# Scores of the differential attention as matmuls over 64 rows, two maps on the two halves of TensorE's rows

## The chip, the cores and the metric

The kernel runs on one core of a Trainium2 chip. The metric is the device time of one execution in microseconds; the time before is the median of three runs, 740.84 us (739.97 to 741.19). All tensors are float32; matmuls take float32 operands rounded to the type fp32r.

## What is computed

One encoder block over 512 tokens of width 1024: a joint projection, two attentions side by side, gates, an output projection, a SwiGLU channel mixer and a final norm. The change touches the second attention, which has 4 heads with two maps each, of 64 dimensions:

```python
bq = apply_rope(bq.reshape(b, s, B_HEADS, 2, HEAD_DIM).transpose(0, 2, 3, 1, 4), ang_1d)
bk = apply_rope(bk.reshape(b, s, B_HEADS, 2, HEAD_DIM).transpose(0, 2, 3, 1, 4), ang_1d)
...
sc = jnp.einsum('bhcqd,bhcsd->bhcqs', qi, k).astype(jnp.float32) * scale
p = jax.nn.softmax(sc, axis=-1)
diff = (p[:, :, 0] - lam * p[:, :, 1]).astype(v.dtype)
return jnp.einsum('bhqs,bhse->bhqe', diff, v)
```

The index c is the map. Each score is a product over 64 numbers, and there are 2 x 512 x 512 scores for each head.

## The kernel before

To keep accuracy, an operand is split into a high part (rounded to fp32r, on ScalarE, line 73) and a low part (the rest, on VectorE, line 80). A projection takes three matmuls for each block: high by high, high by low, low by high (`mm3`, lines 93 to 95).

`group_b(h)` makes one head of the second attention. It loads four units of weights, and for each of four token tiles (128 tokens) it projects to 384 columns (128 of q, 128 of k, 128 of v; tile `acc_b`), scales into `z`, splits v, applies the rotary embedding and packs q and k with `pack_heads`. A packed row holds for each of q map 0, q map 1, k map 0, k map 1 the 64 high and the 64 low numbers side by side, and for k a third part, the unsplit 64 numbers again (line 247). TensorE transposes these pieces of 128 columns (line 254, tile `pt_b`): q as high over low, k once as high over low and once as low over whole. That is six transposes for each token tile, in two PSUM tiles of four and two, and three copies to SBUF on ScalarE (line 256).

`attend_b(h)` goes over the four token tiles. `probs` makes one map's scores of 128 queries by 512 keys with two matmuls over all 128 rows (line 353): the first adds high by high and low by low, the second high by low and low by high. Then come the maximum (VectorE, line 355), the exponential with its sum (ScalarE, line 358) and the reciprocal (line 360). Tiles `sc_b_0x` to `sc_b_3x` are the first map's scores of the four token tiles, `sc_b_0y` to `sc_b_3y` the second map's. All scores share two PSUM banks (`ps_sc`), so a score matmul waits until the exponential of the tile two scores earlier has read its bank. The two maps are joined, the result is transposed (line 366, `ptp_b`), split and multiplied with v (`mm3`, tile `ob`).

The heads are woven: `attend_b(0)` runs with `group_b(2)`, `attend_b(1)` with `group_b(3)`, `attend_b(2)` and `attend_b(3)` with the gate columns (`gate_col`, tile `gt`, matmuls of 512 columns), while the first attention (`attend_a`) has `group_b(1)` and two gate columns between its heads. The program text is not the order of execution: a scheduler that works with a simulated timeline draws the order of each engine's queue, and TensorE then runs its queue strictly in that order.

Of the kernel before, what the change touches and what calls it, by code (L numbers as in the profile page):

```python
# [37 lines left out]
def kernel(  # L38
# [33 lines left out]
    def split_hi(dst, src):  # L72
        a.copy(dst, src)  # L73
# [5 lines left out]
    def split_lo(dst, src, hi):  # L79
        v.tensor_tensor(out=dst, in0=src, in1=hi.bitcast(F32), op=ALU.subtract)  # L80
# [122 lines left out]
    def do_rope(q4, tab, tt, nm):  # L203
        cos_, sin_ = tab
        n, nh = q4.shape[1], q4.shape[2]
        w = n * nh * HD

        def flat(tag):
            t = tmp.tile([P, S], F32, tag=tag, name=f"{tag}_{nm}")[:, :w]
            return t, t.rearrange("p (n h d) -> p n h d", h=nh, d=HD)  # L210

        def bc(t, c):
            return t[:, tt:tt + n, c].unsqueeze(2).to_broadcast([P, n, nh, c.stop - c.start])

        r, r4 = flat("t1")
        t, t4 = flat("t2")
        v.tensor_tensor(out=r4, in0=q4, in1=bc(cos_, slice(0, HD)), op=ALU.mult)
        for h in range(2):
            c, o = slice(32 * h, 32 * h + 32), slice(32 - 32 * h, 64 - 32 * h)
            g.tensor_tensor(out=t4[:, :, :, c], in0=q4[:, :, :, o], in1=bc(sin_, c), op=ALU.mult)  # L220
        v.tensor_tensor(out=r, in0=r, in1=t, op=ALU.add)
        return r.rearrange("p (h d) -> p h d", d=HD)
# [14 lines left out]
    def u_tile(nm, dt=F32R, shape=(P, 2, S)):  # L237
        return up.tile(list(shape), dt, tag="u", name=nm)

    def pack_heads(r3, nh, nk, nm):  # L240
        qs = tmp.tile([P, 8 * P], F32R, tag="qs", name=f"qs_{nm}")
        w = 3 * HD if nk else P
        qs = qs[:, :nh * w].rearrange("p (h w) -> p h w", w=w)
        split_hi(qs[:, :, 0:HD], r3)
        split_lo(qs[:, :, HD:P], r3, qs[:, :, 0:HD])
        if nk:
            v.tensor_copy(qs[:, nh - nk:, P:], r3[:, nh - nk:, :])
        return qs

    def transpose_heads(srcs, dsts, tt, nm, av=False):  # L250
        pt = ps_av.tile([P, S], F32, tag="av", name=f"pt_{nm}") if av else ps_hd.tile([P, S], F32, tag="hd", name=f"pt_{nm}")
        ptr = pt.bitcast(F32R)
        for j, src in enumerate(srcs):
            pe.transpose(out=ptr[:, j * P:(j + 1) * P], in_=src, identity=identr)
        for i, dst in enumerate(dsts):
            a.copy(dst[:, :, tt * P:(tt + 1) * P], pt[:, 2 * i * P:(2 * i + 2) * P].rearrange("p (j t) -> p j t", t=P))

    def pair(qs, h):
        return [qs[:, h, 0:P], qs[:, h, HD:HD + P]]
# [65 lines left out]
    def group_b(h, parts):  # L325
        us = [load_unit(w_in[6 + 4 * h + u, :, :768], f"b{h}_{u}", 768) for u in range(4)]
        vt = u_tile(f"vb{h}", shape=(P, NT, 2, P))
        qT = u_tile(f"qTb{h}")
        kT = [u_tile(f"kTb{h}_{i}") for i in range(2)]
        for tt in range(NT):  # L330
            nm = f"b{h}_{tt}"
            t = slice(tt * P, (tt + 1) * P)
            acc = ps_mm.tile([P, S], F32, tag="mm", name=f"acc_{nm}")[:, :384]
            for kt in range(KT):
                hi, lo = us[kt // 2]
                o = (kt % 2) * 384
                mm3(acc, xgh[:, kt, t], xgl[:, kt, t], hi[:, o:o + 384], lo[:, o:o + 384], kt == 0, kt == KT - 1)
            z = tmp.tile([P, S], F32, tag="q", name=f"z_{nm}")
            a.activation(z[:, :128], acc[:, :128], AF.Copy, scale=rstd8[:, tt:tt + 1])
            a.activation(z[:, 128:384], acc[:, 128:384], AF.Copy, scale=rstd[:, tt:tt + 1])  # L340
            split_hi(vt[:, tt, 0, :], z[:, 256:384])
            split_lo(vt[:, tt, 1, :], z[:, 256:384], vt[:, tt, 0, :])
            qs = pack_heads(do_rope(z[:, :256].rearrange("p (n h d) -> p n h d", n=1, d=HD), tabs["b"], tt, nm), 4, 2, nm)
            transpose_heads([qs[:, 0, 0:P], qs[:, 1, 0:P]] + pair(qs, 2), [qT, kT[0]], tt, f"{nm}_0")
            transpose_heads(pair(qs, 3), [kT[1]], tt, f"{nm}_1")
            if tt == NT - 1:
                parts[:] = [qT, kT, vt]
            yield True

    def probs(ql, kT, tt, nm):  # L350
        sc = ps_sc.tile([P, S], F32, tag="sc", name=f"sc_{nm}")
        for i in range(2):
            pe.matmul(sc, lhsT=ql[:, tt * P:(tt + 1) * P], rhs=kT[:, i, :], start=i == 0, stop=i == 1)
        nm_ = small.tile([P, 1], F32, tag="nmax", name=f"nmax_{nm}")
        v.tensor_reduce(out=nm_, in_=sc, op=ALU.max, axis=AX.X, negate=True)  # L355
        pr_ = pp.tile([P, S], F32, tag="p", name=f"p_{nm}")
        s_ = small.tile([P, 1], F32, tag="psum", name=f"s_{nm}")
        a.activation(pr_, sc, AF.Exp, bias=nm_, scale=1.0, accum_out=s_)  # L358
        r_ = small.tile([P, 1], F32, tag="prec", name=f"r_{nm}")
        v.reciprocal(out=r_, in_=s_)  # L360
        return pr_, r_
# [11 lines left out]
    def attend_a(qT, kT, vt, fillers):  # L373
        for h in range(8):
            kv = h // 4
            if h >= 2:
                fillers[h - 2]()
            ps = []
            for tt in range(NT):
                nm = f"a{h}_{tt}"  # L380
                p_, r_ = probs(qT[h // 2][:, h % 2, :], kT[kv], tt, nm)
                g.tensor_scalar(out=p_, in0=p_, scalar1=r_, scalar2=1.0, op0=ALU.mult, op1=ALU.mult)  # L382
                ps.append(p_)
            av = ps_av.tile([P, S], F32, tag="av", name=f"oa_{h}")
            for kt in range(NT):
                ph, pl = transpose_p(ps, kt, f"a{h}_{kt}")
                pe.matmul(av, lhsT=vt[:, kt, kv, :], rhs=ph, start=kt == 0, stop=False)
                pe.matmul(av, lhsT=vt[:, kt, kv, :], rhs=pl, start=False, stop=kt == NT - 1)
            if h % 4 == 0:
                oA.append(u_tile(f"oA{kv}", F32))  # L390
            low = tmp.tile([HD, S], F32, tag="avt", bufs=1, name=f"low_{h}")
            a.copy(low, av[HD:P, :])
            v.tensor_tensor(out=oA[kv][HD * (h % 2):HD * (h % 2) + HD, h % 4 // 2, :], in0=av[0:HD, :], in1=low, op=ALU.add)

    def attend_b(h, qT, kT, vt):
        ps = []
        for tt in range(NT):
            nm = f"b{h}_{tt}"
            p0, r0 = probs(qT[:, 0, :], kT[0], tt, nm + "x")
            g.tensor_scalar(out=p0, in0=p0, scalar1=r0, scalar2=1.0, op0=ALU.mult, op1=ALU.mult)  # L400
            p1, r1 = probs(qT[:, 1, :], kT[1], tt, nm + "y")
            c1 = small.tile([P, 1], F32, tag="c1", name=f"c1_{nm}")
            v.tensor_tensor(out=c1, in0=r1, in1=nlam, op=ALU.mult)
            v.scalar_tensor_tensor(out=p0, in0=p1, scalar=c1, in1=p0, op0=ALU.mult, op1=ALU.add)
            ps.append(p0)
            yield True
        av = ps_av.tile([P, S], F32, tag="av", name=f"ob_{h}")
        for kt in range(NT):
            ph, pl = transpose_p(ps, kt, f"b{h}_{kt}")
            mm3(av, vt[:, kt, 0, :], vt[:, kt, 1, :], ph, pl, kt == 0, kt == NT - 1)  # L410
            yield True
        if h % 2 == 0:
            oB.append(u_tile(f"oB{h // 2}", F32))
        o = oB[h // 2][:, h % 2, :]
        a.copy(o, av)
        sq = tmp.tile([P, S], F32, tag="avt", bufs=1, name=f"sqb_{h}")
        a.activation(sq, av, AF.Square)
        pn = ps_tp.tile([P, S], F32, tag="tp", name=f"pn_{h}")
        for tt in range(NT):
            pe.matmul(pn[:, tt:tt + 1], lhsT=sq[:, tt * P:(tt + 1) * P], rhs=ones, start=True, stop=True)  # L420
        rs = small.tile([P, NT], F32, tag="rsb", name=f"rsb_{h}")
        rsqrt_mean(rs, pn[:, 0:NT], P, NT)
        pb = ps_tp.tile([P, S], F32, tag="tp", name=f"pb_{h}")
        for tt in range(NT):
            pe.matmul(pb[:, tt * P:(tt + 1) * P], lhsT=rs[:, tt:tt + 1].to_broadcast([P, P]), rhs=ident, start=True, stop=True)
        v.scalar_tensor_tensor(out=o, in0=o, scalar=gsub, in1=pb, op0=ALU.mult, op1=ALU.mult)
# [579 lines left out]
```

## Time and profile before

| | |
|---|---|
| median of three runs | 740.84 us |
| profiled execution | 741.09 us |
| its span, first to last instruction | 739.3 us |
| matmuls on TensorE | 4335 |
| mean granted clock of TensorE | 0.993 |
| VectorE, ScalarE, GpSimd busy | 545.3, 420.0, 174.3 us |

The second attention's scores run between 160 and 280 us of the span, its projections and transposes between 76 and 255 us. A busy time in the profile counts each matmul from its start to its modelled end, and consecutive matmuls overlap; what one costs in a full queue is read from the distance between starts.

### The profile page before, as it was taken

Reading aid. Unit: us, or ns where it says so; the run is one execution under the profiler, and the core shown is the slowest. Engines: PE = TensorE matmul, PEld = TensorE weight load, DVE = VectorE, ACT = ScalarE, POOL = GpSimd, SP = SyncE. Lnnn points to the kernel's source line nnn. Section 1 sums busy time; section 2 is a strip of 40 time slices with the busy share of each in tenths; the row PEclk is TensorE's granted clock in tenths of the full one; section 3 lists DMA queues with packets and bytes.
Section 4 is the critical chain, followed back from the end, with each engine's and each line's share of the span. In section 5 each row is a group of like instructions: output and inputs, shape, how many; then the busy total and the mean of one; then the engine's idle time right before and its main releaser. Section 6 shows DMA issues by size and latency. Waiting matters only on the chain.

```text
span 739.3 us, 11815 instructions
## 1 busy us (share of the span) xinstructions
PE 717.8 (97%) x4335; PEld 644.3 (87%) x4335; DVE 545.3 (74%) x917; ACT 420.0 (57%) x755; POOL 174.3 (24%) x223
## 2 busy tenths in 40 slices
PE   5899999999999999999999999999999999999996
PEld 5789978789998888888889989999999999988885
DVE  5787778859987565557447967878887888778884
ACT  6355687967677666432326635555555555546672
POOL 3656433335662220100000022211212120110002
PEclk9899999999999999999999999999999999999999
DMA  8215708068979652433413397876687773559973
GB/s 315 94 44 184 244 22 271 21 133 197 235 171 244 139 138 72 152 107 112 143 58 106 98 317 217 242 207 178 215 253 194 234 184 125 172 180 321 339 241 115
DMA packets 48634, 129.95 MB, mean 176 GB/s; under 512 B 5600, under 2 KB 6496, under 8 KB 48576
## 3 DMA queue, kind: packets, MB, share of 16 engines
q1 hardware_dynamic: 34736, 95.57, 38.0%
q0 software_dynamic: 11248, 28.19, 19.5%
q10 hardware_dynamic: 2592, 5.45, 2.1%
q8 instruction: 34, 0.56, 0.3%
q14 instruction: 24, 0.20, 0.1%
HBM read 119.87 MB, written 32.37 MB: 206 GB/s over the span
## 4 chain that ended last, share of the span: by engine, by line
PE 92%; DMA 3%; DVE 2%; ACT 1%; issue 1%; SPq 0%; POOL 0%; POOLq 0%; ACTq 0%; DVEq 0%
PE q L95 5%; PE q L94 5%; PE q L93 5%; PE gt L94 4%; PE gt L93 4%; PE gt L95 4%; PE p L95 4%; PE p L93 4%; PE p L94 4%; PE acc_b L93 3%; PE acc_b L94 3%; PE acc_b L95 3%; PE r L94 2%; PE r L93 2%; PE r L95 2%; PE pp L93 2%
## 5 line engine op out<-in xcount | busy, mean ns | idle before, releaser
L95 PE MATMUL gt<-xgh,wlo_g 128*128 128x512 f32 x128 | 50.6, 395 | 0.0
L94 PE MATMUL gt<-xgl,whi_g 128*128 128x512 f32 x128 | 50.5, 394 | 0.0
L93 PE MATMUL gt<-xgh,whi_g 128*128 128x512 f32 x128 | 50.4, 394 | 0.0
L691 POOL DMA_DIRECT2D x<-in_w_x_dram x18 | 16.2, 899 | 126.5 <-DMA x<-in_w_x_dram 53.9
L94 PE MATMUL acc_b<-wlo_b,xgh 128*128 128x384 f32 x128 | 43.6, 340 | 0.0
L93 PE MATMUL acc_b<-whi_b,xgh 128*128 128x384 f32 x128 | 43.5, 340 | 0.0
L95 PE MATMUL acc_b<-whi_b,xgl 128*128 128x384 f32 x128 | 43.4, 339 | 0.0
L768 POOL DMA_DIRECT2D sd<-s x44 | 28.2, 670 | 51.6 <-DVE s L765 24.8
L382 POOL TENSOR_SCALAR p_a<-p_a,r_a 128x512 f32<-128x512 f32 x32 | 23.6, 740 | 51.1 <-DVE r_a L360 43.6
L73 ACT CAST whi_a<-raw_a 128x1024 fp32r<-128x1024 f32 x18 | 18.9, 1050 | 21.1 <-issue 11.7
L80 DVE TENSOR_TENSOR wlo_t<-raw_t,whi_t 128x1024 fp32r<-128x1024 f32 (+1 forms) x24 | 27.0, 1130 | 4.0 <-ACT whi_t L73 3.9
L73 ACT CAST sh<-sr 128x512 fp32r<-128x512 f32 (+1 forms) x30 | 17.5, 583 | 21.6 <-PE p L94 7.8
L73 ACT CAST whi_y<-y 128x1024 fp32r<-128x1024 f32 x18 | 18.9, 1050 | 19.1 <-PE p2d L95 15.4
L93 PE MATMUL p<-whi_t,sh 128*128 128x512 f32 (+1 forms) x77 | 27.4, 360 | 1.0 <-DVE x L860 1.0
L80 DVE TENSOR_TENSOR wlo_y<-y,whi_y 128x1024 fp32r<-128x1024 f32 x18 | 22.0, 1221 | 8.7 <-ACT whi_y L73 8.7
L95 PEld LDWEIGHTS gt<-xgh,wlo_g 128*128 128x128 f32 x128 | 24.0, 188 | 4.8
L94 PEld LDWEIGHTS gt<-xgl,whi_g 128*128 128x128 f32 x128 | 24.0, 188 | 4.8
L93 PEld LDWEIGHTS gt<-xgh,whi_g 128*128 128x128 f32 x128 | 24.1, 188 | 4.8
L358 ACT ACTIVATE p_a<-sc_a,nmax_a 128x512 f32<-128x512 f32 x32 | 22.5, 703 | 8.8 <-DVE nmax_a L355 7.9
L94 PE MATMUL p<-wlo_t,sh 128*128 128x512 f32 (+1 forms) x77 | 26.9, 359 | 0.0
L220 POOL TENSOR_TENSOR t_b<-z_b,csb 128x128 f32<-128x128 f32 x32 | 23.8, 763 | 11.6 <-ACT z_b L340 10.1
L95 PE MATMUL p<-whi_t,sl 128*128 128x512 f32 (+1 forms) x77 | 26.1, 360 | 0.1
(390 smaller groups left out, 2734.2 us busy)
## 6 DMA issues: line engine op xcount, KB each, us to landing
td<-in_w_down_dram SPq DMA_DIRECT2D x20, 512.0 KB, 8.1
raw_t<-td SPq DMA_DIRECT2D x20, 512.0 KB, 4.6
x<-in_w_x_dram SPq DMA_DIRECT2D x18, 512.0 KB, 4.9
raw_a<-in_w_gu_dram SPq DMA_DIRECT2D x18, 512.0 KB, 5.1
x<-in_w_x_dram POOLq DMA_DIRECT2D x18, 512.0 KB, 5.9
raw_g<-in_w_in_dram SPq DMA_DIRECT2D x16, 512.0 KB, 6.1
sr<-sd SPq DMA_DIRECT2D x25, 256.0 KB, 4.4
raw_b<-in_w_in_dram SPq DMA_DIRECT2D x16, 384.0 KB, 3.8
```

The source lines that it names most:

```text
L73: a.copy(dst, src)
L80: v.tensor_tensor(out=dst, in0=src, in1=hi.bitcast(F32), op=ALU.subtract)
L93: pe.matmul(acc, lhsT=lh, rhs=rh, start=start, stop=False, skip_group_check=loose)
L94: pe.matmul(acc, lhsT=lh, rhs=rl, start=False, stop=False, skip_group_check=loose)
L95: pe.matmul(acc, lhsT=ll, rhs=rh, start=False, stop=stop, skip_group_check=loose)
L220: g.tensor_tensor(out=t4[:, :, :, c], in0=q4[:, :, :, o], in1=bc(sin_, c), op=ALU.mult)
L358: a.activation(pr_, sc, AF.Exp, bias=nm_, scale=1.0, accum_out=s_)
L382: g.tensor_scalar(out=p_, in0=p_, scalar1=r_, scalar2=1.0, op0=ALU.mult, op1=ALU.mult)
L691: g.dma_start(x, w_x1[f], accum_op=ALU.add)
L768: g.dma_start(sdram[i][p][:, k, :], t)
```

## The change

`pack_heads` is no longer used for the second attention. `pack_pairs` packs the two maps side by side: 128 columns of high parts (64 of map 0, 64 of map 1) and 128 of low parts, for q and for k. Transposed, map 0 lies on rows 0 to 63 and map 1 on rows 64 to 127. Four transposes in one PSUM tile and two copies are left for each token tile, and k has one tile instead of two. `scores_pair` takes both score banks and makes the scores of both maps with three matmuls each over 64 rows: high by high, high by low, low by high; it writes them in turn, map 0, map 1, map 0 and so on. Low by low is no longer computed. `probs` is split so that it takes a finished score tile.

```diff
--- before.py
+++ after.py
@@ -245,6 +245,16 @@
         split_lo(qs[:, :, HD:P], r3, qs[:, :, 0:HD])
         if nk:
             v.tensor_copy(qs[:, nh - nk:, P:], r3[:, nh - nk:, :])
+        return qs
+
+    def pack_pairs(r3, nh, nm):
+
+        qs = tmp.tile([P, 8 * P], F32R, tag="qs", name=f"qs_{nm}")[:, :2 * nh * HD]
+        qs = qs.rearrange("p (s j w) -> p s j w", s=2, w=P)
+        r3 = r3.rearrange("p (j h) d -> p j h d", h=2)
+        hi, lo = (qs[:, i].rearrange("p j (h d) -> p j h d", d=HD) for i in range(2))
+        split_hi(hi, r3)
+        split_lo(lo, r3, hi)
         return qs
 
     def transpose_heads(srcs, dsts, tt, nm, av=False):
@@ -326,7 +336,7 @@
         us = [load_unit(w_in[6 + 4 * h + u, :, :768], f"b{h}_{u}", 768) for u in range(4)]
         vt = u_tile(f"vb{h}", shape=(P, NT, 2, P))
         qT = u_tile(f"qTb{h}")
-        kT = [u_tile(f"kTb{h}_{i}") for i in range(2)]
+        kT = u_tile(f"kTb{h}")
         for tt in range(NT):
             nm = f"b{h}_{tt}"
             t = slice(tt * P, (tt + 1) * P)
@@ -340,17 +350,28 @@
             a.activation(z[:, 128:384], acc[:, 128:384], AF.Copy, scale=rstd[:, tt:tt + 1])
             split_hi(vt[:, tt, 0, :], z[:, 256:384])
             split_lo(vt[:, tt, 1, :], z[:, 256:384], vt[:, tt, 0, :])
-            qs = pack_heads(do_rope(z[:, :256].rearrange("p (n h d) -> p n h d", n=1, d=HD), tabs["b"], tt, nm), 4, 2, nm)
-            transpose_heads([qs[:, 0, 0:P], qs[:, 1, 0:P]] + pair(qs, 2), [qT, kT[0]], tt, f"{nm}_0")
-            transpose_heads(pair(qs, 3), [kT[1]], tt, f"{nm}_1")
+            qs = pack_pairs(do_rope(z[:, :256].rearrange("p (n h d) -> p n h d", n=1, d=HD), tabs["b"], tt, nm), 4, nm)
+            transpose_heads([qs[:, i % 2, i // 2, :] for i in range(4)], [qT, kT], tt, nm)
             if tt == NT - 1:
                 parts[:] = [qT, kT, vt]
             yield True
 
-    def probs(ql, kT, tt, nm):
+    def scores(ql, kT, tt, nm):
         sc = ps_sc.tile([P, S], F32, tag="sc", name=f"sc_{nm}")
         for i in range(2):
             pe.matmul(sc, lhsT=ql[:, tt * P:(tt + 1) * P], rhs=kT[:, i, :], start=i == 0, stop=i == 1)
+        return sc
+
+    def scores_pair(qT, kT, tt, nms):
+
+        scs = [ps_sc.tile([P, S], F32, tag="sc", name=f"sc_{nm}") for nm in nms]
+        for n, (i, j) in enumerate(((0, 0), (0, 1), (1, 0))):
+            for c in range(2):
+                r = slice(HD * c, HD * (c + 1))
+                pe.matmul(scs[c], lhsT=qT[r, i, tt * P:(tt + 1) * P], rhs=kT[r, j, :], start=n == 0, stop=n == 2)
+        return scs
+
+    def probs(sc, nm):
         nm_ = small.tile([P, 1], F32, tag="nmax", name=f"nmax_{nm}")
         v.tensor_reduce(out=nm_, in_=sc, op=ALU.max, axis=AX.X, negate=True)
         pr_ = pp.tile([P, S], F32, tag="p", name=f"p_{nm}")
@@ -378,7 +399,7 @@
             ps = []
             for tt in range(NT):
                 nm = f"a{h}_{tt}"
-                p_, r_ = probs(qT[h // 2][:, h % 2, :], kT[kv], tt, nm)
+                p_, r_ = probs(scores(qT[h // 2][:, h % 2, :], kT[kv], tt, nm), nm)
                 g.tensor_scalar(out=p_, in0=p_, scalar1=r_, scalar2=1.0, op0=ALU.mult, op1=ALU.mult)
                 ps.append(p_)
             av = ps_av.tile([P, S], F32, tag="av", name=f"oa_{h}")
@@ -396,9 +417,10 @@
         ps = []
         for tt in range(NT):
             nm = f"b{h}_{tt}"
-            p0, r0 = probs(qT[:, 0, :], kT[0], tt, nm + "x")
+            sc0, sc1 = scores_pair(qT, kT, tt, (nm + "x", nm + "y"))
+            p0, r0 = probs(sc0, nm + "x")
             g.tensor_scalar(out=p0, in0=p0, scalar1=r0, scalar2=1.0, op0=ALU.mult, op1=ALU.mult)
-            p1, r1 = probs(qT[:, 1, :], kT[1], tt, nm + "y")
+            p1, r1 = probs(sc1, nm + "y")
             c1 = small.tile([P, 1], F32, tag="c1", name=f"c1_{nm}")
             v.tensor_tensor(out=c1, in0=r1, in1=nlam, op=ALU.mult)
             v.scalar_tensor_tensor(out=p0, in0=p1, scalar=c1, in1=p0, op0=ALU.mult, op1=ALU.add)
```

On TensorE, at the first scores of head 0, two score matmuls of a map stand among the projection's matmuls before (the second map's two follow some twenty rows later):

```order
L95 MATMUL acc_b_0_2082<-whi_b_1_2062,xgl 128x384
L93 MATMUL acc_b_0_2082<-whi_b_1_2062,xgh 128x384
L353 MATMUL sc_b_0x<-kTb_0_706,qTb_705 128x512 x2
L94 MATMUL acc_b_0_2082<-wlo_b_1_2063,xgh 128x384
L95 MATMUL acc_b_0_2082<-whi_b_1_2062,xgl 128x384
L93 MATMUL acc_b_0_2082<-whi_b_2_2068,xgh 128x384
L94 MATMUL acc_b_0_2082<-wlo_b_2_2069,xgh 128x384
L95 MATMUL acc_b_0_2082<-whi_b_2_2068,xgl 128x384
```

and after the change (line 371 is in `scores_pair`):

```order
L93 MATMUL acc_b_0_2041<-whi_b_1_2022,xgh 128x384
L94 MATMUL acc_b_0_2041<-wlo_b_1_2023,xgh 128x384
L371 MATMUL sc_b_0x<-kTb_706,qTb_705 128x512 x3
L95 MATMUL acc_b_0_2041<-whi_b_1_2022,xgl 128x384
L93 MATMUL acc_b_0_2041<-whi_b_1_2022,xgh 128x384
L94 MATMUL acc_b_0_2041<-wlo_b_1_2023,xgh 128x384
L371 MATMUL sc_b_0y<-kTb_706,qTb_705 128x512 x3
L95 MATMUL acc_b_0_2041<-whi_b_1_2022,xgl 128x384
```

Three matmuls of one map stand together, then three of the projection, then three of the other map; the two maps do not alternate here.

On TensorE, at the first scores of head 1, before:

```order
L353 MATMUL sc_b_0x<-kTb_0_1129,qTb_1128 128x512 x2
L93 MATMUL acc_b_0_2492<-whi_b_0_2466,xgh 128x384
L94 MATMUL acc_b_0_2492<-wlo_b_0_2467,xgh 128x384
L95 MATMUL acc_b_0_2492<-whi_b_0_2466,xgl 128x384
L93 MATMUL acc_b_0_2492<-whi_b_0_2466,xgh 128x384
L94 MATMUL acc_b_0_2492<-wlo_b_0_2467,xgh 128x384
L95 MATMUL acc_b_0_2492<-whi_b_0_2466,xgl 128x384
L93 MATMUL acc_b_0_2492<-whi_b_1_2472,xgh 128x384
L94 MATMUL acc_b_0_2492<-wlo_b_1_2473,xgh 128x384
L353 MATMUL sc_b_0y<-kTb_1_1130,qTb_1128 128x512 x2
```

and after:

```order
L387 MATMUL ptp_b_1_2326<-ident,p_b_1x 128x128
L387 MATMUL ptp_b_1_2326<-ident,p_b_2x 128x128
L371 MATMUL sc_b_0x<-kTb_1108,qTb_1107 128x512
L371 MATMUL sc_b_0y<-kTb_1108,qTb_1107 128x512
L371 MATMUL sc_b_0x<-kTb_1108,qTb_1107 128x512
L371 MATMUL sc_b_0y<-kTb_1108,qTb_1107 128x512
L371 MATMUL sc_b_0x<-kTb_1108,qTb_1107 128x512
L371 MATMUL sc_b_0y<-kTb_1108,qTb_1107 128x512
L93 MATMUL acc_b_0_2438<-whi_b_0_2413,xgh 128x384
```

Here the six matmuls of the two maps stand directly behind one another and alternate.

On TensorE, the transposes of packed q and k (`pt_b`, `qs_b`); before, in the stage of the first attention, a group of two for one token tile and a group of four for the next:

```order
L353 MATMUL sc_a_2_1204<-kTa_242,qTa_553 128x512 x2
L254 MATMUL pt_b_2_1_857<-identr,qs_b_2_846 128x128 x2
L387 MATMUL oa_1055<-ph_a_0_1061,va 128x512
L353 MATMUL sc_a_3_1215<-kTa_242,qTa_553 128x512 x2
L254 MATMUL pt_b_3_0_901<-identr,qs_b_3_897 128x128 x4
L388 MATMUL oa_1055<-pl_a_0_1062,va 128x512
```

and after, for the first token tile of head 2 (`ptp_a` are transposes of the first attention's probabilities):

```order
L95 MATMUL acc_b_1_2115<-whi_b_3_2034,xgl 128x384
L264 MATMUL pt_b_0_2080<-identr,qs_b_0_2077 128x128
L387 MATMUL ptp_a_2_1898<-ident,p_a_0_1836 128x128
L387 MATMUL ptp_a_2_1898<-ident,p_a_1_1847 128x128
L387 MATMUL ptp_a_2_1898<-ident,p_a_2_1858 128x128
L387 MATMUL ptp_a_2_1898<-ident,p_a_3_1869 128x128
L93 MATMUL acc_b_2_2189<-whi_b_0_2016,xgh 128x384
L264 MATMUL pt_b_0_2080<-identr,qs_b_0_2077 128x128 x3
```

The group of two is gone; the group of four that is left stands here as one and three, with other work between.

## Rows read from the trace of the kernel before

**Rows 1.** The page, parts 1, 2 and 4: busy share, granted clock in tenths, ending chain.
```profile
PE 717.8 (97%) x4335; PEld 644.3 (87%) x4335; DVE 545.3 (74%) x917; ACT 420.0 (57%) x755; POOL 174.3 (24%) x223
...
PEclk9899999999999999999999999999999999999999
...
PE 92%; DMA 3%; DVE 2%; ACT 1%; issue 1%; SPq 0%; POOL 0%; POOLq 0%; ACTq 0%; DVEq 0%
```

**Rows 2.** Windows of 40 us: busy us of each engine, clock, DMA share.
```profile
core 0: us, PE busy (x) PEld busy (x) DVE busy (x) ACT busy (x) POOL busy (x), PEclk, DMA share, GB/s
80.00:120.00 40.00, 38.78 (x224) 34.00 (x223) 31.49 (x68) 29.38 (x76) 15.35 (x22) 1.00 0.36 120
120.00:160.00 40.00, 38.83 (x213) 31.24 (x212) 29.13 (x62) 31.97 (x71) 13.40 (x19) 1.00 0.47 126
160.00:200.00 40.00, 39.95 (x234) 37.36 (x233) 33.67 (x76) 29.52 (x68) 21.87 (x27) 1.00 0.88 207
200.00:240.00 40.00, 40.00 (x219) 34.77 (x219) 31.36 (x66) 29.23 (x63) 17.14 (x20) 1.00 0.95 208
240.00:280.00 40.00, 40.00 (x202) 33.45 (x202) 23.58 (x43) 24.80 (x43) 9.06 (x11) 1.00 0.62 136
```

**Rows 3.** Waits of TensorE, 80 to 200 us: total us, times, longest.
```profile
PE sc_a L353 <- ACT p_a L358: 1.5, 3, 0.6
PE oa L387 <- ACT ph_a L73: 0.7, 1, 0.7
```

**Rows 4.** Line 353, first and last of eight score tiles: ns min/median/max, first and last start.
```profile
L353 PE MATMUL sc_b_0x<-kTb,qTb x8: 390/397/478, 160.6 to 254.9; 128*128 128x512 f32 x8
...
L353 PE MATMUL sc_b_3y<-kTb,qTb x8: 387/392/398, 182.3 to 279.5; 128*128 128x512 f32 x8
```

**Rows 5.** TensorE in order of time, 278.8 to 279.8 us: start, length, instruction.
```profile
278.83 0.63 PE L353 MATMUL sc_b_3x<-kTb,qTb 128*128 128x512 f32 x2
279.30 0.62 PE L353 MATMUL sc_b_3y<-kTb,qTb 128*128 128x512 f32 x2
279.76 0.40 PE L93 MATMUL gt<-xgh,whi_g 128*128 128x512 f32 x1
```

**Rows 6.** Weight loads in order of time, 279.5 to 279.8 us.
```profile
279.53 0.19 PEld L93 LDWEIGHTS gt<-xgh,whi_g 128*128 128x128 f32 x1
279.76 0.19 PEld L94 LDWEIGHTS gt<-xgl,whi_g 128*128 128x128 f32 x1
```

**Rows 7.** Groups by line (count, busy us, mean ns, idle before): transposes and copies.
```profile
L254 PE MATMUL pt_b<-identr,qs_b 128*128 128x128 f32 x96 | 12.7, 241 | 0.0
...
L256 ACT CAST kTb<-pt_b 128x256 fp32r<-128x256 f32 x32 | 12.5, 390 | 5.0 <-PE pt_b L254 5.0
...
L256 ACT CAST qTb<-pt_b 128x256 fp32r<-128x256 f32 x16 | 6.1, 384 | 5.4 <-PE pt_b L254 5.4
```

**Rows 8.** Line 247, the extra copy of k: ns min/median/max, first and last start.
```profile
L247 DVE CAST qs_b<-t_b x16: 206/216/649, 76.1 to 236.9; 128x128 fp32r<-128x128 f32 x16
```

**Rows 9.** TensorE in order of time around a group of four transposes.
```profile
229.01 0.46 PE L254 MATMUL pt_b<-identr,qs_b 128*128 128x128 f32 x4
229.31 0.46 PE L95 MATMUL gt<-xgh,wlo_g 128*128 128x512 f32 x1
229.61 0.40 PE L93 MATMUL gt<-xgh,whi_g 128*128 128x512 f32 x1
```

**Rows 10.** TensorE in order of time around a group of two transposes.
```profile
254.46 0.28 PE L254 MATMUL pt_b<-identr,qs_b 128*128 128x128 f32 x2
254.59 0.70 PE L353 MATMUL sc_b_0x<-kTb,qTb 128*128 128x512 f32 x2
255.12 0.40 PE L93 MATMUL gt<-xgh,whi_g 128*128 128x512 f32 x1
```

**Rows 11.** Lines 355 and 358 for one score tile: ns min/median/max, starts.
```profile
L355 DVE TENSOR_REDUCE nmax_b_0x<-sc_b_0x x4: 671/676/693, 161.5 to 255.3; 128x1 f32<-128x512 f32 x4
...
L358 ACT ACTIVATE p_b_0x<-sc_b_0x,nmax_b_0x x4: 684/687/689, 165.1 to 257.1; 128x512 f32<-128x512 f32 x4
```

## The prediction

> **What bounds the kernel now.** I read the page's first and fourth parts first. TensorE is busy for 717.8 of 739.3 us, and 92% of the chain that ended last is TensorE's own work [rows 1]. The kernel is one queue of matmuls, and every matmul added to or taken from that queue shows in the time unless a wait beside it changes too. Next I read the windows of the stage that the change touches, 80 to 280 us: from 200 us on TensorE is busy in all of each 40 us, at a granted clock of 1.00, while VectorE, ScalarE and GpSimd each have at least 8 us to spare in every 40 [rows 2]. Only in 80 to 160 us is there a gap, 1.22 + 1.17 = 2.4 us. The view of waits names its largest parts: scores of the first attention that wait for ScalarE's exponentials (1.5 us) and one product that waits for a split (0.7 us) [rows 3].
>
> A busy time is not what a matmul costs the queue. Each of the eight score tiles' matmuls of 512 columns is shown as about 0.39 us long [rows 4], but in the order of time the pair of one map starts at 278.83, the pair of the other at 279.30 and the next matmul at 279.76, so two cost 0.46 to 0.47 and one costs 0.23 us [rows 5]. I call this a slot. The rest, 0.39 - 0.23 = 0.16 us, is the tail of one matmul under the head of the next. The weights of each are loaded under the matmul before: the load shown at 279.53 belongs to the matmul that starts at 279.76 [rows 5, 6].
>
> **The change, part by part.** First, the transposes. Before, each of the 16 token tiles (4 heads by 4) has a group of four and a group of two, 96 in all [rows 7]. Four cost 229.31 - 229.01 = 0.30 us, and the matmul behind them takes another 0.07 us (229.31 to 229.61 is 0.30 against a slot of 0.23) [rows 9]; two cost 254.59 - 254.46 = 0.13 us, and the two score matmuls behind them take 0.53 instead of 0.46 us, again 0.07 more [rows 10]. A transpose of 128 columns is too short to cover the next load of weights. After the change there are 64 transposes: 32 fewer at 0.07 us are 2.2 us. The groups don't halve, though: the new order splits seven of the groups of four into one and three, so there are 23 runs instead of 32, and 9 x 0.07 = 0.6 us goes with them. Together -2.8 us, on the path, because TensorE is the path.
>
> Second, the score matmuls. Before there are 64 (16 tiles, two maps, two each): 64 slots. Afterwards there are 96, each over 64 rows: for each map high by high, high by low and low by high, the low-by-low product being dropped. Two of them can share a slot only if one stands on each half of the rows and they are next to each other in the queue. The code writes them in turn, but the scheduler does not keep that: I counted 29 runs of score matmuls in the new queue. In seven of the sixteen pairs other matmuls stand between all three of one map and all three of the other. If neighbours on different halves share a slot and everything else is in order, a run of three of one map is 3 slots, six in turn are 3, three and then three directly behind are 5. Over the four heads this gives 22 + 21 + 20 + 15 = 78 slots, 14 more than 64: 14 x 0.23 = +3.2 us. If none share, it is 96: 32 x 0.23 = +7.4 us. If all did, 48: -3.7 us; this queue can't give that, with those seven pairs apart.
>
> The Trainium skill, TensorE: Matmul & The Clock Gate, Part 3 (Packing small matmuls), says that matmuls on different row groups run at the same time but start and end in program order. No row of this trace shows a matmul over part of the rows, so sharing is open here. By that rule the sum takes the 78.
>
> Third, the price of going from the whole array to its halves and back. The 29 runs lie among matmuls over 128 rows, so there are 58 such changes where there were none. The trace before has no row for one. From below: nothing, since going from transposes to products and back costs no more than the uncovered load [rows 9, 10]. From above: if the queue lets the tail run out each time, 0.16 us [rows 4, 5], 58 x 0.16 = +9.3 us. I also can't exclude a gain at a boundary, but a shared slot is the only one I can name and it is counted already. I take 0.07 us, the one extra that these rows show when a matmul's load isn't hidden by the one before: 58 x 0.07 = +4.1 us. Both ends stay in the range.
>
> The Trainium skill, TensorEngine Tiling (Array Packing), section Key Properties, says that changing the tiling mode, not just the tile, drains TensorE. It gives no figure. This is the rule that speaks against the change; the rows neither show nor deny it. With it the sum takes the upper end, without it the lower.
>
> Fourth, the other engines. ScalarE loses one of its three copies out of each tile's transposes: 16 x 0.39 = 6.2 us; VectorE loses 16 casts of 0.22 us, 3.5 us [rows 7, 8]. The splits keep their shapes. I cost this at nothing where TensorE is full (from 200 us on). Half of it falls before 160 us, into the stretch with the 2.4 us gap, and might shorten it. SP's queue holds the same transfers in the same order as before, so no load of weights is moved.
>
> Fifth, the new wait. Both score banks are taken at once: where the two maps stand in turn, the second matmul waits for the previous exponential of the other map, and everything behind it in TensorE's queue (projection, products) waits too. Before, the same bank waits exist one map at a time, and in 160 to 280 us the score matmuls of this attention nearly never stopped for one (0.05 us of gap in 120 us [rows 2]). In the new queue one map's runs of neighbouring tiles stand 24 to 45 rows apart, over 4 us at 0.17 to 0.23 us a row, and the bank needs a maximum of 0.68 us and an exponential of 0.69 us in that time [rows 11], twice that when the other map's come first. I put it at nothing; each miss would cost some tenths, as the mean of 0.5 us (1.5 us in three waits) in [rows 3].
>
> **The sum**, against the profiled execution's own 741.09 us (span 739.3 and 1.8 around it; the median of the runs is 740.84, 0.25 lower): -2.8 + 3.2 + 4.1 = +4.5 us. Put on the median: 740.84 + 4.5 = 745.3 us. With the price per change between 0.03 and 0.16 us this case runs from 743 to 750.5.
>
> **The rivals.**
> No sharing: the two halves don't run at the same time (or not for this type), and the changes of mode are free. Then +7.4 - 2.8 = +4.6 us, 745.4 us. For it: the trace shows no two matmuls that ever start together. Against it: each load already runs under another matmul and is shorter than a slot (0.19 against 0.23 us) [rows 5, 6], so the load of the second half need not hold it back. The time is almost that of my forecast, so only the trace will part the two. If there is no sharing and a price as well, it is 749.5 to 755.
>
> Sharing and free changes: 3.2 - 2.8 = +0.4 us, 741.2 us, no change that can be told. For it: transposes and products of different kinds already alternate in this queue at little cost [rows 9]. Against it: none of those change the rows in use.
>
> The other side: the changes of mode are free and the waits on ScalarE in 80 to 160 us go. One mechanism: ScalarE has some 3 us less to do before 160 us, the exponentials come earlier, and the stops of the first attention's scores vanish. The gap is 2.4 us in the busy view, and each of the four stops also hides a tail of 0.16, so up to 3.0 us: 741.2 - 3.0 = 738.2 us at best, and 739.7 with half of it. It makes the kernel faster by more than 1.5 us only if a change of mode costs under (3.0 - 0.4 - 1.5) / 58 = 0.02 us. For it: ScalarE is the one that TensorE waits for [rows 3]. Against it: it has 8 to 10.6 us to spare in each 40 us there [rows 2], so the waits come from the order rather than from the load, and the order is drawn anew.
>
> **How the numbers follow.** A measurement of this kernel can tell about 0.2% from no change, 1.5 us. Chances: forecast (sharing, priced changes) 0.38; no sharing, free 0.12; no sharing and priced 0.05; sharing and free, nothing else 0.26; the waits go 0.19. The first three end slower, except for the cheapest end of the forecast (0.02), and the fourth is slower once in ten: 0.36 + 0.12 + 0.05 + 0.03 = 0.56 slower. The fifth gives faster in two thirds of its cases (0.13) and the fourth in a fifth of its (0.05): 0.18 faster. The remaining 0.26 is no change. The range from 738.3 to 750.5 holds all of these but the whole price together with no sharing (0.05), the forecast's dearest end and an order whose waits shift further than the gap shown, under 2 in 10 together. The forecast's own range is 743 to 750.5.
>
> **What would show it.** In the trace after, a run of six in turn should show pairs of starts close together and 3 slots in all (0.7 us) if sharing works, 1.4 us if not. At the edges of each run the distance to the next start shows the price directly: 0.23 us means free, 0.30 my value, 0.39 or more a full drain. Transposes should cost 0.30 per four, and 64 of them be left. The windows from 200 to 280 us should still show TensorE full, and the granted clock at 1.00. I am wrong if the edges read 0.23 us, if half-height matmuls in one half cost less than a slot, or if the gap of 80 to 160 us moves by more than 2 us either way.

## The result, and the profile after

The changed kernel takes 753.51 us (median of four runs, 752.15 to 754.77) against 740.44 us of the kernel before: a ratio of 1.017, 95% interval 1.0157 to 1.0183, 13.1 us slower. The forecast was slower, but 745.3 us, and the range ended at 750.5. The profiled execution took 754.77 us with a span of 753.0, 13.7 us more than the 739.3 before. All accounts below are between spans.

From the page of the changed kernel, parts 1 and 4, the lines that answer to [rows 1]:

```profile
PE 730.2 (97%) x4335; PEld 642.2 (85%) x4335; DVE 542.0 (72%) x901; ACT 414.6 (55%) x739; POOL 170.0 (23%) x223
...
PE 90%; DMA 3%; ACT 2%; DVE 2%; issue 2%; SPq 0%; POOL 0%; POOLq 0%; ACTq 0%; DVEq 0%
```

TensorE has as many matmuls as before (32 transposes fewer, 32 score matmuls more) and is busy 12.4 us longer; it still is the path. The windows, which answer to [rows 2], show more:

```profile
80.00:120.00 40.00, 38.60 (x225) 33.54 (x224) 31.75 (x67) 30.90 (x79) 14.66 (x23) 1.00 0.33 111
120.00:160.00 40.00, 38.18 (x195) 29.80 (x194) 27.54 (x58) 27.99 (x60) 13.99 (x19) 1.00 0.48 134
160.00:200.00 40.00, 40.00 (x216) 33.03 (x215) 29.45 (x64) 27.15 (x62) 16.03 (x21) 1.00 0.77 178
200.00:240.00 40.00, 40.00 (x204) 31.90 (x203) 28.19 (x59) 23.64 (x56) 17.39 (x23) 0.96 0.85 180
240.00:280.00 40.00, 40.00 (x190) 30.03 (x189) 21.77 (x38) 24.93 (x35) 7.28 (x9) 1.00 0.71 159
```

Three things are to be seen. From 160 us on TensorE is shown as full, yet it gets fewer matmuls done in the same 40 us (216, 204 and 190 against 234, 219 and 202) and its loads are busy less: it is slower, not waiting. The gap before 160 us has grown from 2.4 to 1.40 + 1.82 = 3.2 us. And between 200 and 240 us the mean granted clock is 0.96.

Where the slowness sits is read in order of time. TensorE around the first run of three half-height matmuls:

```profile
160.43 0.34 PE L94 MATMUL acc_b<-wlo_b,xgh 128*128 128x384 f32 x1
160.69 0.96 PE L371 MATMUL sc_b_0x<-kTb,qTb 64*128 64x512 f32 x3
161.58 0.44 PE L95 MATMUL acc_b<-whi_b,xgl 128*128 128x384 f32 x1
161.86 0.34 PE L93 MATMUL acc_b<-whi_b,xgh 128*128 128x384 f32 x1
162.04 0.33 PE L94 MATMUL acc_b<-wlo_b,xgh 128*128 128x384 f32 x1
```

and the loads of weights in the same stretch:

```profile
160.25 0.19 PEld L94 LDWEIGHTS acc_b<-wlo_b,xgh 128*128 128x128 f32 x1
160.69 0.53 PEld L371 LDWEIGHTS sc_b_0x<-kTb,qTb 64*128 64x128 f32 x3 [0.25 <-issue]
161.58 0.19 PEld L95 LDWEIGHTS acc_b<-whi_b,xgl 128*128 128x128 f32 x1 [0.37 <-issue]
161.69 0.19 PEld L93 LDWEIGHTS acc_b<-whi_b,xgh 128*128 128x128 f32 x1
```

In a full queue a matmul of 384 columns takes 0.18 us to the next start and one of 512 takes 0.23. Here the step onto the run is 160.69 - 160.43 = 0.26, 0.08 late; the run and the step off it take 161.58 - 160.69 = 0.89 instead of 0.69, 0.20 late; and the next step takes 0.28, 0.10 late. Together about 0.4 us for one run, 0.2 us for each change of rows. The loads point at the reason: in a full queue a load starts with the matmul before the one it is for ([rows 6]; 160.25 here for the matmul of 160.43). In the trace before, 4318 of 4335 loads start ahead of their own matmul; in this one, at all 58 changes of rows, the load starts with its own matmul, here at 160.69 and again at 161.58, after an idle time of 0.25 and 0.37 us that no engine caused ("issue"). Read this way both things are lost: the overlap with the tail of the matmul before, and the head start of the load. How the 0.20 us divide between the two is a reading of these rows; no run separates them.

The two halves do share. TensorE in the changed kernel around a run of six in turn:

```profile
191.79 0.50 PE L371 MATMUL sc_b_0x<-kTb,qTb 64*128 64x512 f32 x1
191.80 0.50 PE L371 MATMUL sc_b_0y<-kTb,qTb 64*128 64x512 f32 x1
192.13 0.39 PE L371 MATMUL sc_b_0x<-kTb,qTb 64*128 64x512 f32 x1
192.13 0.39 PE L371 MATMUL sc_b_0y<-kTb,qTb 64*128 64x512 f32 x1
192.37 0.39 PE L371 MATMUL sc_b_0x<-kTb,qTb 64*128 64x512 f32 x1
192.37 0.39 PE L371 MATMUL sc_b_0y<-kTb,qTb 64*128 64x512 f32 x1
192.69 0.44 PE L93 MATMUL acc_b<-whi_b,xgh 128*128 128x384 f32 x1
```

Starts come in pairs within 0.01 us, and the six take 0.90 us: three slots and the price at the edges.

**The account.** Counted in this order of time there are 29 runs and 73 slots, not 78. Transposes -2.8 (still the forecast's value); slots (73 - 64) x 0.23 = +2.1; edges 29 x 0.40 = +11.6; the gap before 160 us +0.8; the stretch at the lower clock +1.7 (below). The sum is +13.4 of the 13.7 us measured.

**The lower clock.** TensorE near 218 us:

```profile
216.30 0.95 PE L442 MATMUL pn<-ones,sqb 128*128 128x1 f32 x8
217.11 0.52 PE L264 MATMUL pt_b<-identr,qs_b 128*128 128x128 f32 x4
217.56 1.15 PE L371 MATMUL sc_b_3y<-kTb,qTb 64*128 64x512 f32 x3
218.65 0.69 PE L93 MATMUL acc_b<-whi_b,xgh 128*128 128x384 f32 x1
...
221.05 0.52 PE L94 MATMUL acc_b<-wlo_b,xgh 128*128 128x384 f32 x1
221.37 0.44 PE L95 MATMUL acc_b<-whi_b,xgl 128*128 128x384 f32 x1
221.65 0.34 PE L93 MATMUL acc_b<-whi_b,xgh 128*128 128x384 f32 x1
```

From about 218.2 to 221.6 us a matmul of 384 columns takes 0.32 us to the next start (221.05 to 221.37) instead of 0.18: the lower of the two clocks, 1.2 GHz, for 3.4 us, in which half of the work gets done, so 1.7 us are lost. Before it stand eight matmuls of one column, four transposes and a run over half the rows.

### The profile page after: what moved, and what is told of

It is laid out like the page before. It is cut to its first block, busy times and chain, and to the rows that moved or that the text cites. A ratio compares the mean times of both kernels' runs of the same rounds, so it can differ in the third digit from the quotient of the medians.

```text
span 753.0 us, 11778 instructions
## 1 busy us (share of the span) xinstructions
PE 730.2 (97%) x4335; PEld 642.2 (85%) x4335; DVE 542.0 (72%) x901; ACT 414.6 (55%) x739; POOL 170.0 (23%) x223
## 4 chain that ended last, share of the span: by engine, by line
PE 90%; DMA 3%; ACT 2%; DVE 2%; issue 2%; SPq 0%; POOL 0%; POOLq 0%; ACTq 0%; DVEq 0%
PE q L95 5%; PE q L94 5%; PE q L93 5%; PE gt L93 4%; PE gt L95 4%; PE gt L94 4%; PE p L95 4%; PE p L93 4%; PE p L94 4%; PE acc_b L93 3%; PE acc_b L95 3%; PE acc_b L94 3%; PE r L94 2%; PE r L95 2%; PE r L93 2%; PE pp L93 2%
## 5 line engine op out<-in xcount | busy, mean ns | idle before, releaser
L790 POOL DMA_DIRECT2D sd<-s x44 | 28.6, 678 | 51.8 <-DVE s L787 25.0
L220 POOL TENSOR_TENSOR t_b<-z_b,csb 128x128 f32<-128x128 f32 x32 | 20.3, 653 | 33.9 <-ACT z_b L350 31.3
L73 ACT CAST whi_g<-raw_g 128x1024 fp32r<-128x1024 f32 x16 | 16.7, 1049 | 18.8 <-PE gt L94 13.3
```

Source lines behind the costliest of these rows:

```text
L790: g.dma_start(sdram[i][p][:, k, :], t)
```

## The experiments

Ten runs were made. Where a time is compared, the kernel before ran beside it (740.35 to 740.71 us).

### The changed kernel again

> The changed kernel itself, profiled a second time. If the stretch of 3.4 us at the lower clock (1.2 GHz) near 218 us belongs to this kernel's queue, it is there again at the same work; if it is chance, it is elsewhere or missing, and the span is about 1.7 us shorter.

It took 754.72 us with the same span, 753.0, and the lower clock came at the same work: the mean of 200 to 240 us is 0.96 again, and the matmuls of 0.32 us stand behind the same eight one-column matmuls, transposes and run. Two profiles of two show it at the same work, so it belongs to this queue, as far as two can tell.

### The same queue over all rows

```diff
-                r = slice(HD * c, HD * (c + 1))
+                r = slice(0, P)
```

> The changed kernel, but each of the 96 score matmuls reads all 128 rows instead of 64 (so each score is the sum over both maps, and the two maps' scores are alike). The scheduler draws the same 29 runs. Theory (a change between matmuls over 128 and over 64 rows costs about 0.2 us, 0.40 us for a run of score matmuls): the 29 x 0.40 = 11.6 us go, the sharing of slots goes too, 96 - 64 = 32 slots x 0.23 = +7.3, transposes -2.8: about 745 us, and distances at the edges of a run of 0.23 us. Rival (the time comes from the new order of the queue and its waits on the two score banks, whatever the rows): 751 us or more, edges unchanged or waits in the view of waits.

745.96 us, ratio 1.0078 (1.0063 to 1.0093): within 1 us of the theory's 745, 5 us under the rival's 751. The first run of scores in this kernel, with what stands around it:

```profile
160.59 0.33 PE L94 MATMUL acc_b<-wlo_b,xgh 128*128 128x384 f32 x1
160.76 0.86 PE L371 MATMUL sc_b_0x<-kTb,qTb 128*128 128x512 f32 x3
161.46 0.33 PE L95 MATMUL acc_b<-whi_b,xgl 128*128 128x384 f32 x1
161.63 0.34 PE L93 MATMUL acc_b<-whi_b,xgh 128*128 128x384 f32 x1
```

The step on is 0.17, the run 0.70 and the step off 0.17 us: no price at an edge. With 23 slots more than the changed kernel and the same 29 runs, it is 7.6 us faster, and the clock of 200 to 240 us is 1.00. The gap before 160 us is 3.2 us here too, so its 0.8 us are the share of the new order. The rest of what made the changed kernel slow came with the half-height matmuls and went with them, in this profile the stretch at the lower clock too.

### One half-height matmul in each gate column of the kernel before

```diff
-            mm3(acc, hi[:, c], lo[:, c], xgh[:, kt, :], xgl[:, kt, :], kt == 0, kt == KT - 1)
+            r = slice(0, HD) if kt == 3 else slice(0, P)
+            pe.matmul(acc, lhsT=hi[:, c], rhs=xgh[:, kt, :], start=kt == 0, stop=False)
+            pe.matmul(acc, lhsT=hi[r, c], rhs=xgl[r, kt, :], start=False, stop=False)
+            pe.matmul(acc, lhsT=lo[:, c], rhs=xgh[:, kt, :], start=False, stop=kt == KT - 1)
```

> The kernel before, with one of the 24 matmuls of each of the 16 gate columns over 64 rows instead of 128 (half of that one product's low part is left out). The queue's order, the slots and the transposes stay. Theory (price per change of rows): 16 runs of one, 16 x 0.40 = +6.4 us, 746.8 us, with 0.32 us ahead of the half-height matmul, 0.43 behind it and 0.33 for the next. Rival (the score banks or the new order are to blame): 740.5 us, no difference. Rival (price per half-height matmul, 0.12 us): 742.4 us.

747.43 us, ratio 1.0097 (1.0082 to 1.0112): +7.1 us against 6.4 expected, where the rivals asked for nothing or for 1.9. (Of the 0.7 us between, 0.4 lie ahead of the first edited matmul in the profile: the first projection of the second attention starts at 52.61 instead of 52.22 us.) This is the disputed price by itself, without new scores, transposes or order. TensorE around one of the sixteen:

```profile
246.04 0.39 PE L440 MATMUL gt<-xgh,whi_g 128*128 128x512 f32 x1
246.35 0.50 PE L441 MATMUL gt<-xgl,whi_g 64*128 64x512 f32 x1
246.78 0.50 PE L442 MATMUL gt<-xgh,wlo_g 128*128 128x512 f32 x1
247.12 0.39 PE L440 MATMUL gt<-xgh,whi_g 128*128 128x512 f32 x1
```

The steps are 0.31, 0.43 and 0.34 us where 0.23 was due: 0.08 + 0.20 + 0.11 = 0.39 us. A matmul that does half the work costs nearly three slots.

### Three half-height matmuls in each gate column

```diff
-            mm3(acc, hi[:, c], lo[:, c], xgh[:, kt, :], xgl[:, kt, :], kt == 0, kt == KT - 1)
+            r = slice(0, HD) if kt == 3 else slice(0, P)
+            mm3(acc, hi[r, c], lo[r, c], xgh[r, kt, :], xgl[r, kt, :], kt == 0, kt == KT - 1)
```

> The kernel before, with all three matmuls of one of the eight blocks of each of the 16 gate columns over 64 rows (half of that block's product is left out): three times as many half-height matmuls as in the kernel with one, in 16 to 20 runs. Theory (price per change of rows): 6.4 to 8 us over before, 747 to 748.5 us, as with one. Rival (price per half-height matmul): 3 x 7 = 21 us, 761 us.

748.90 us, ratio 1.0108 (1.0094 to 1.0121). The 48 matmuls stand in 20 runs, 20 x 0.40 = 8.0 us, and 8.2 were measured. Inside a run the second step is a plain slot (246.62 to 246.86):

```profile
246.29 0.49 PE L93 MATMUL gt<-xgh,whi_g 64*128 64x512 f32 x1
246.62 0.39 PE L94 MATMUL gt<-xgl,whi_g 64*128 64x512 f32 x1
246.86 0.39 PE L95 MATMUL gt<-xgh,wlo_g 64*128 64x512 f32 x1
247.18 0.50 PE L93 MATMUL gt<-xgh,whi_g 128*128 128x512 f32 x1
```

The price is one of the change, not of the matmul.

### Six in a run

```diff
...
-        scs = [ps_sc.tile([P, S], F32, tag="sc", name=f"sc_{nm}") for nm in nms]
+        both = ps_two[0].tile([P, 2, S], F32, tag="sc", name=f"sc_{nms[0]}")
+        scs = [both[:, c, :] for c in range(2)]
...
-                pe.matmul(scs[c], lhsT=qT[r, i, tt * P:(tt + 1) * P], rhs=kT[r, j, :], start=n == 0, stop=n == 2)
+                with tc.high_priority():
+                    pe.matmul(scs[c], lhsT=qT[r, i, tt * P:(tt + 1) * P], rhs=kT[r, j, :], start=n == 0, stop=n == 2)
...
+    sc_a.close()
+    ps_two = [pool(attn, "ps_two", space=PSUM)]
     weave(gen, steps(todo[2:4]))
```

> The changed kernel with the two score banks of a pair as one tile of two banks (taken and given back together) and a higher priority for the six matmuls, so that they stand directly in turn: 16 runs of six instead of 29 runs. Theory (price per run): 16 x 0.40 = +6.4, 48 slots instead of 64 = -3.7, transposes -2.8: about 740.5 us, plus what waits for the banks add (0 to 3 us). Rival (price per half-height matmul, 11.6 us over 96 of them): the same 96 matmuls keep it, with 25 slots fewer than the changed kernel 747 us or more. Rival (order and waits): 750 us or more, since the banks are freed later than before.

753.33 us, ratio 1.0163 (1.0136 to 1.019): a miss by 13 us (10 beyond the expectation's upper end), and by the time alone the rivals would have it. By the trace, only the second has a part in it, and not for the reason it gave: no score matmul waits for its banks. There are 16 runs of three slots, and their edges cost 0.4 us as everywhere. So the price is one of the run here too. What came on top are stops and what follows them:

```profile
211.14 0.98 PE L374 MATMUL sc_b_2x<-kTb,qTb 64*128 64x512 f32 x6
214.65 1.86 PE L445 MATMUL pn<-ones,sqb 128*128 128x1 f32 x8 [2.53 <-ACT sqb L442]
216.37 0.73 PE L265 MATMUL pt_b<-identr,qs_b 128*128 128x128 f32 x4
218.47 0.80 PE L93 MATMUL gt<-xgh,whi_g 128*128 128x512 f32 x1 [1.37 <-ACT z_b L351]
219.06 0.63 PE L94 MATMUL gt<-xgl,whi_g 128*128 128x512 f32 x1
219.49 0.63 PE L95 MATMUL gt<-xgh,wlo_g 128*128 128x512 f32 x1
```

The redrawn queue has TensorE wait for ScalarE (the square for the norm, then a projection's copy), and from the end of the first stop on it is at the lower clock for 10.2 us, the second stop among them (0.43 us from 219.06 to 219.49). The windows show the sum of it:

```profile
200.00:240.00 40.00, 36.10 (x180) 29.33 (x179) 26.54 (x53) 21.63 (x50) 12.64 (x17) 0.87 0.79 172
280.00:320.00 40.00, 37.61 (x190) 29.93 (x188) 21.93 (x38) 23.32 (x35) 4.72 (x6) 1.00 0.37 100
```

Idle time 3.9 + 2.4 us, half of the 12.2 us of work at the lower clock (10.2 + 3.4 less the stop of 1.4) 6.1, the gap before 160 us +0.8: 13.2, and with the -0.1 expected of slots, edges and transposes +13.1 of the 13.8 us measured. The runs are priced as expected; the expectation of 0 to 3 us for waits was wrong. The four executions spread from 754.98 to 750.87 us as their mean granted clock goes from 0.984 to 0.991, and this account is of the slowest.

### Three of one map, then three of the other

```diff
...
-        for n, (i, j) in enumerate(((0, 0), (0, 1), (1, 0))):
-            for c in range(2):
+        for c in range(2):
+            for n, (i, j) in enumerate(((0, 0), (0, 1), (1, 0))):
...
+                if c or n:
+                    tc.keep_in_program_order(m)
```

> The kernel with six score matmuls in a run, but queued as three of the first map and then three of the second instead of in turn. If TensorE starts matmuls strictly in the order of its queue, the second map's first one can share only with the first map's third: five slots in a run, some 1.15 us between the first start and the last end of slots, 16 x 2 x 0.23 = +7.3 us against the same kernel in turn. If each half has its own order, the starts come in pairs as before: three slots, no difference.

750.86 us in one run at a mean clock of 0.991, the same as the kernel with six in turn at that clock (750.87), and not the 7.3 us over it that a strict order asks for. A run and the next matmul:

```profile
250.34 0.97 PE L374 MATMUL sc_b_2x<-kTb,qTb 64*128 64x512 f32 x6
251.24 0.50 PE L93 MATMUL gt<-xgh,whi_g 128*128 128x512 f32 x1
```

Six take 0.90 us, three slots with edges, as in turn, in all 16 runs; five would be 1.36. So the second map's matmuls start beside the first map's although they are queued behind all three. Both maps share one tile name here. With names it is seen by holding the changed kernel against the one over all rows: TensorE starts the same 4335 matmuls in the same order in both but for eight places, all of them in runs of scores. In the kernel over all rows, where none share, two runs of six are three and three:

```profile
244.15 0.84 PE L371 MATMUL sc_b_3x<-kTb,qTb 128*128 128x512 f32 x3
244.83 0.84 PE L371 MATMUL sc_b_3y<-kTb,qTb 128*128 128x512 f32 x3
```

In the changed kernel the same six start at 251.28 (x), 251.29 (y), 251.62 (x), 251.63 (y), 251.85 (x) and 251.86 (y). So what is said of the queue ahead of the prediction, that TensorE runs it strictly in its order, fits what these traces show of matmuls over all rows, but not of matmuls on different halves. A shorter run in the changed kernel shows the same: in the queue stand two of map x and then one of map y, and they start as x, y, x.

```order
L371 MATMUL sc_b_1x<-kTb_2437,qTb_2436 128x512
L93 MATMUL ob_3019<-ph_b_1_3071,vb_2038 128x512
L371 MATMUL sc_b_1x<-kTb_2437,qTb_2436 128x512 x2
L371 MATMUL sc_b_1y<-kTb_2437,qTb_2436 128x512
L94 MATMUL ob_3019<-pl_b_1_3072,vb_2038 128x512
```

```profile
274.15 0.49 PE L93 MATMUL ob<-ph_b,vb 128*128 128x512 f32 x1
274.58 0.49 PE L371 MATMUL sc_b_1x<-kTb,qTb 64*128 64x512 f32 x1
274.58 0.49 PE L371 MATMUL sc_b_1y<-kTb,qTb 64*128 64x512 f32 x1
274.91 0.39 PE L371 MATMUL sc_b_1x<-kTb,qTb 64*128 64x512 f32 x1
```

### The new packing alone

```diff
-        for n, (i, j) in enumerate(((0, 0), (0, 1), (1, 0))):
+        for n, (i, j) in enumerate(((0, 0), (0, 1))):
...
-                r = slice(HD * c, HD * (c + 1))
+                r = slice(0, P)
```

> The changed kernel's packing, four transposes and two copies for each token tile, but the scores with two matmuls over all 128 rows for each map, as many slots as before (so each score is the sum over both maps of high by high and high by low). Theory (TensorE is the path, and the transposes are worth what their distances in the queue say): -2.8 us, 737.7 us. Rival (what the shorter transposes give is lost to waits on the score banks or on ScalarE in the first attention's stage): 740 us or more.

741.91 us, ratio 1.0019 (1.0009 to 1.0028): the rival's result, though only part of the loss lies where it looked. TensorE stops twice around the output projection's start, for 1.74 us together (the square for the norm, then a split), runs 3.4 us at the lower clock from the second stop on (another 1.6), and the gap before 160 us is 0.8 us larger.

Single profiles need care here: the mean granted clock of the first 40 us, ahead of everything edited, is 0.96 in this one and 0.91 in the kernel before (the lower level near 20 us lasts half as long), and its first projection of the second attention starts at 51.16 instead of 52.22 us. From there on it is 1.8 us longer than the kernel before. All transposes, with what the matmul behind a group takes beyond its slot, are 3.3 us cheaper; idle time is 2.4 us more, the tails and loads that the stops uncover 1.1, the lower clock 1.6.

### Four transposes without half-height matmuls

```diff
...
-            transpose_heads([qs[:, 0, 0:P], qs[:, 1, 0:P]] + pair(qs, 2), [qT, kT[0]], tt, f"{nm}_0")
-            transpose_heads(pair(qs, 3), [kT[1]], tt, f"{nm}_1")
+            pt = transpose_heads([qs[:, i, :] for i in range(4)], [qT, kT[0]], tt, nm)
+            k2 = pt[:, 2 * P:].rearrange("p (j t) -> p j t", t=P)
+            v.tensor_copy(swap[0:HD, :, t], k2[HD:P])
+            v.tensor_copy(swap[HD:P, :, t], k2[0:HD])
...
```

> The kernel before with its scores as they are (two matmuls over 128 rows for each map), but only four transposes for each token tile: k is transposed once as high over low, and the second form (low over high) is made from the same bank by two copies of 64 rows on VectorE that cross to the other half, instead of two more transposes and a copy. Nothing stands over 64 rows on TensorE. Theory (TensorE is the path, its transposes are worth their distances, only the change of rows made the changed kernel slow): 32 transposes and 16 uncovered loads fewer, 32 x 0.07 + 16 x 0.07 = 3.4 us, 737.0 us, less what the redrawn order adds in waits (0 to 3 us). Rival (VectorE is the next limit: 16 x 0.5 us more work on it): 741 us or more, with waits of TensorE for VectorE.

743.98 us, ratio 1.0045 (1.0033 to 1.0057): slower, 4 us over the theory's upper end and in the rival's range. The rival's waits for VectorE are there before 160 us (idle 3.5 instead of 2.4 us), but they are the smaller part: here too TensorE stops around the start of the output projection (1.7 us), and the clock falls there:

```profile
280.00:320.00 40.00, 38.26 (x184) 31.38 (x183) 18.89 (x28) 18.38 (x23) 3.64 (x3) 0.96 0.34 119
```

To test that last part, the last gate column was queued behind the last head's products, so that TensorE has work while the square is made:

```diff
...
-    for f in todo[13:]:
+    for f in todo[13:15]:
         f()
+    with tc.issue_after(last_ob[0].ins):
+        todo[15]()
```

> As the one with the filler, but both swapping copies on VectorE as in the first kernel of that kind: it differs from that one in the place of the last gate column alone. Theory (stop and lower clock before the output projection cost 3.4 us): 744 - 3.4 = 740.5 us. Rival (they cost nothing, since the loss comes back elsewhere): 744 us.

740.68 us, ratio 1.000 (0.9991 to 1.0009): 3.3 us less than without the filler, as expected, and the window shows the clock mended and 0.5 us of idle time instead of 1.7. (The profiles alone would not do for this: in the first 40 us the one with the filler has a mean clock of 0.96, the other 0.91.)

```profile
280.00:320.00 40.00, 39.46 (x198) 32.89 (x197) 18.60 (x27) 18.14 (x23) 3.66 (x3) 1.00 0.33 119
```

With one of the two copies on ScalarE instead (the kernel that the expectation above calls "the one with the filler"):

> The kernel with four transposes and swapping copies (scores over 128 rows), one of the two swapping copies on ScalarE and one on VectorE, and the last gate column queued on TensorE behind the last head's products, so that TensorE has 5.5 us of work while the square for the norm is made. Theory (what the 3.4 us of transposes gave was lost to the stop before the norm, 1.7 us, and the stretch at the lower clock behind it, 1.7 us): both go, 740.5 us or less; 738 us if the first attention's stage stays as in the kernel before. Rival (the losses lie elsewhere, in the work added to VectorE and ScalarE): 743 us or more.

741.87 us, ratio 1.0017 (1.0008 to 1.0026), between the two expectations, with 2.9 us of waits for ScalarE's exponentials in place of the waits for VectorE. No version beat the kernel before: what the transposes give, the stops of the redrawn order, waits for the added copies among them, take back.

## Why the prediction was wrong

**The direction and the mechanism were right**: half-height matmuls share a slot, the transposes shrink, and the price of changing between whole and half rows outweighs both.

**The step that failed is the third, the price of a change.** The forecast took 0.07 us, bounded by 0.16 us above, because it counted the lost tail and the uncovered load as alternatives. As the loads read, both are lost at a change: the matmul starts 0.09 us late, and its neighbour another 0.11 us late because the load could not begin before. Two changes cost 0.40 us (shown in place, by the gate columns with one and with three, and by its absence in the same queue over all rows). 58 x 0.20 = 11.6 us stand where the forecast had 4.1 and its dearest case 9.3. This alone moves the forecast to 752.8 us, past the end of the range. The sign that was named for it looked at one step, 0.30 us for the forecast's value and 0.39 for a full drain; the price is spread over three steps, and the first of them, 0.31 to 0.32 us onto a run, would have passed for the forecast's.

**The slots** were 73 instead of 78 (+2.1 instead of +3.2 us). The count of runs, 29, was right. The rule used inside a run, strict order, was not: two matmuls share even when others of the same half stand between them in the queue, and three runs that start in another order than over all rows account for the five slots (two, two and one).

**The transposes** were worth somewhat more than -2.8 us. Counted by distances between starts from the first projection of the second attention on, all transposes with what they add to the matmul behind cost 32.0 us before and 28.6 to 28.9 in the five kernels with four per token tile and no half-height matmuls. Against that stands what the sum had at nothing: in each of them TensorE stops more often, and a stop costs its idle time and also the tail and the load that it uncovers, together 2 to 5 us more than before.

**What was costed at nothing** came to 2.5 us in the account of the changed kernel: the gap before 160 us grew by 0.8 us instead of shrinking with ScalarE's lighter load, and the clock fell once more than before, 1.7 us, which no step foresaw. The fifth step held: no score matmul of this attention stopped for its bank long enough to show.

**Of the rivals**, no sharing is refuted by the pairs of starts, free changes by the edges, and the side on which waits go by the gap of 3.2 us. The measured time lies in the range of no sharing with a price (749.5 to 755), but the pairs of starts refute its mechanism: the time alone would have spoken for the wrong one.

By the trace, the new scores could not have paid even in the best order: six half-height matmuls in three slots save one slot of four, 0.23 us, and the run costs 0.40. Over 16 runs that is 2.7 us lost, about what the transposes give.

## What to carry to other kernels

Price a matmul over part of the rows by its run: count the changes between whole and partial rows in the queue as it is drawn, at some 0.2 us each here, before counting shared slots; at 0.40 us a run must save two slots of 0.23 us to pay. Check in the drawn order whether the matmuls that should share stand together at all. And where TensorE is full, an edit beside it is worth what its redrawn queue leaves: two of the versions here lost some 3 us to a stop and the lower clock behind it, and in the one where it was tried, one column of work in the right place gave that back.

## What was not expected of the hardware

- At a change between 128 and 64 rows (all 58 in the changed kernel) the load of weights starts with its own matmul instead of with the one before; 0.20 us a change, 0.39 to 0.40 us for a run of one, three or six.
- Matmuls on different halves keep to an order in each half, not to that of the queue: three and three in the queue start in pairs 0.01 us apart and take 0.90 us with their edges, where strict order asks for 1.36.
- Short stops can be paid twice: behind an idle time of 2.5 us TensorE was at 1.2 GHz for 10.2 us, behind 1.74 us of idle time in two stops at the output projection for 3.4 us. In the changed kernel it fell without a stop, behind one-column matmuls, transposes and a half-height run; with the same queue over all rows it did not. What exactly makes it fall stays open.
